# Loading two neighbouring chunks with one transfer of 64 KB rows in an RMS norm with ReLU

## The chip, the cores and the metric

The kernel runs on one core of a Trainium2 chip. The metric is the device time of one execution in microseconds (us). All runs quoted are with a granted clock of 1.00. The profiled span is the time from the first to the last instruction, some 1.3 us shorter than the device time.

## The reference

```python
def setup_inputs():
    batch, seq, dim = 16, 1024, 512
    x = randn(batch, seq, dim) as float32; gamma = ones(dim); eps = 1e-5

def reference(x, gamma, eps):
    rms = np.sqrt(np.mean(x ** 2, axis=-1, keepdims=True) + eps)
    return np.maximum(x / rms * gamma, 0)
```

There are 16384 rows of 512 numbers: 33.55 MB to read and as much to write.

## The kernel before

The 16384 rows are spread over 128 partitions, 128 rows of `x` on each, and worked off in eight chunks of K = 16 rows per partition (4.19 MB each). There is room for six chunks in the on-chip memory (`slots`), so chunks 6 and 7 go where 0 and 1 were, after those are stored. One queue, that of the issuing engine SP, takes all transfers in the order of this list:

```python
K = 16; G = 8; nslots = 6; room = nslots * K
order = [(L, 0, G), (L, G, G)] + [(L, i * K, K) for i in range(1, nslots)] + [
    (S, 0, K), (S, K, K), (L, room, K), (L, room + K, K),
    (S, 2 * K, 2 * K), (S, 4 * K, 2 * K), (S, room, K), (S, room + K, K)]
blocks = [(0, K), (K, K), (2 * K, 2 * K), (4 * K, 2 * K), (room, K), (room + K, K)]
```

`L` is a load, `S` a store; the numbers are the first row in each partition and the count. `blocks` says how a partition's rows lie in HBM: chunks 4 and 5 form one block, so a partition has 64 KB in one piece there (chunks 2 and 3 form another). Such a piece of one partition, as far as one transfer takes it, is called a row of 16, 32 or 64 KB below, not to be confused with the rows of `x`; it is one descriptor of the transfer and one packet of the profile, which counts 16 small packets more for each transfer's completion. The kernel before stores this block with one transfer of 64 KB rows, but loads it with two transfers of 32 KB rows.

Stores wait for VectorE. Two of them also wait for a count of VectorE's groups (`tick`, raised at the sixth of a group's eight rows). This wait is called the gate here:

```python
if kind == S:
    if order[m - 1][0] == L:
        nc.sync.wait_ge(tick, 6 if a == 0 else 11)
    nc.sync.wait_ge(done, (a + r) // G)
elif a >= room:
    take(nc.sync, sems[order.index((S, a - room, r))], 16)   # wait for the store, then load
transfer(m)
```

GpSimd waits for each load and announces its groups of G = 8 rows to ScalarE:

```python
if kind == L:
    take(nc.gpsimd, sems[m], 16)
    nc.gpsimd.sem_inc(ready, r // G)
```

ScalarE squares and sums each row of a group and takes the root (16 groups, numbered 0 to 15). VectorE takes the reciprocal, multiplies each row by it and by gamma, and clips a group at zero (groups 0 to 11); it does chunks 6 and 7 in two passes over the whole chunk, the second with a custom instruction.

## Time and profile before

| | kernel before |
|---|---|
| device time, median of 3 runs | 160.31 us (160.15 to 160.41) |
| profiled span | 158.9 us |
| VectorE busy | 129.4 us, 81% |
| ScalarE busy | 86.3 us, 54% |
| transfers, share of 16 DMA engines over the span | 98.3% |
| moved | 67.1 MB, 422 GB/s |

The two shares to set against each other are VectorE's and that of the transfers. The page's chain of waits names VectorE, because it follows instructions; whether it or the queue of transfers sets the end is what the prediction had to decide. In the profile's lines DVE is VectorE, ACT ScalarE, POOL GpSimd and SP the issuing engine; a q behind a name is that engine's sequencer, and L117 is line 117 of the kernel. ScalarE's waits of the kernel before (engine, line, what it waited for: us in total, times, longest):

```profile
ACT junk L130 <- POOLq L117: 17.4, 4, 10.4
```

POOLq L117 is GpSimd's announcement. The longest of the four waits, 10.4 us, is the one for chunk 6.

### The profile page before, as it was taken

How to read it: one execution, taken by the hardware profiler on the slowest of the kernel's cores; microseconds unless marked ns; L12 is line 12 of the kernel's file. 1: busy time of each engine (PE TensorE's matmuls, PEld its weight loads, DVE VectorE, ACT ScalarE, POOL GpSimd, SP SyncE). 2: the span in 40 equal slices, each digit the busy share in tenths (PEclk: the TensorE clock that was granted, in tenths of full speed). 3: DMA queues.
4: the chain of work that ended last, by engine and by line, in shares of the span. 5: the costliest groups of instructions: out<-in, count | busy, mean ns of one | idle time of the engine just before them, and what ended most of it. 6: DMA issues, size and time to landing. Idle time of an engine off the chain costs nothing.

```text
span 158.9 us, 902 instructions
## 1 busy us (share of the span) xinstructions
DVE 129.4 (81%) x128; ACT 86.3 (54%) x273; POOL 0.8 (0%) x6
## 2 busy tenths in 40 slices
DVE  0013999999999999999999999999999999996000
ACT  0388919889889989988930098898600000000000
POOL 1000000000000000000000000000000000000000
DMA  6999999999999999999999999996997998999996
GB/s 194 406 454 449 470 404 396 495 429 396 429 487 404 396 462 462 396 404 495 421 396 404 503 412 396 528 495 297 528 478 313 528 412 379 396 396 503 412 404 264
DMA packets 2168, 67.12 MB, mean 422 GB/s; under 512 B 244, under 2 KB 244, under 8 KB 248
## 3 DMA queue, kind: packets, MB, share of 16 engines
q1 hardware_dynamic: 2160, 67.11, 98.3%
q10 hardware_dynamic: 8, 0.01, 0.0%
HBM read 33.56 MB, written 33.55 MB: 422 GB/s over the span
## 4 chain that ended last, share of the span: by engine, by line
DVE 51%; issue 18%; DVEq 5%; ACT 3%; ACTq 0%; POOLq 0%
DVE slots L153 27%; DVE slots L170 11%; DVE slots L173 11%; DVEq L153 3%; ACT junk L130 3%; DVE rstd L148 1%; DVEq L143 1%; DVEq L148 0%; ACTq L130 0%; DVE rstd L168 0%; DVE slots L160 0%; ACT rms L135 0%; DVEq L162 0%; DVEq L172 0%; ACTq L135 0%
## 5 line engine op out<-in xcount | busy, mean ns | idle before, releaser
L130 ACT ACTIVATE junk<-slots 128x512 f32 x128 | 74.4, 581 | 21.9 <-POOLq L117 17.4
L153 DVE SCALAR_TENSOR_TENSOR slots<-slots,rstd,gamma_sb 128x512 f32 x96 | 64.7, 746 | 1.8 <-DVE rstd L148 1.8
L160 DVE TENSOR_SCALAR slots<-slots x12 | 27.5, 2294 | 0.4
L130 ACT ACTIVATION_READ_ACCUMULATOR junk<-slots x128 | 23.9, 186 | 0.0
L173 DVE CUSTOM_DVE_ANT_1 slots<-slots,gamma_sb 128x8192 f32<-128x8192 f32 x2 | 17.4, 8693 | 0.3
L170 DVE TENSOR_TENSOR slots<-slots,rstd 128x8192 f32<-128x8192 f32 x2 | 17.4, 8692 | 0.1
L148 DVE RECIPROCAL rstd<-rms x12 | 2.3, 195 | 5.4 <-ACT rms L135 5.4
L141 DVE LOAD_MASK_SELECT gamma_sb<-gseed x1 | 0.0, 14 | 8.0 <-DMA gseed<-in_gamma_dram 8.0
L135 ACT ACTIVATE rms<-ss,eps_sb x16 | 4.8, 301 | 1.8
L123 ACT ACT_TABLE_LOAD x1 | 1.3, 1283 | 4.0 <-issue 4.0
L141 DVE STREAM_SHUFFLE gamma_sb<-gseed 128x512 f32<-128x512 f32 x1 | 0.7, 717 | 0.0
L112 POOL MEMSET gseed<- 128x512 f32 x1 | 0.5, 525 | 1.9 <-POOLq L97 1.9
L168 DVE RECIPROCAL rstd<-rms 128x16 f32<-128x16 f32 x2 | 0.5, 246 | 0.0
L203 POOL MEMSET const-bfloat16-1.0<- 128x1 bf16 x1 | 0.1, 101 | 0.0
L203 POOL MEMSET const-uint8-127<- 128x1 uint8 x1 | 0.1, 101 | 0.0
L203 POOL MEMSET const-float32-0.0<- 128x1 f32 x1 | 0.1, 98 | 0.2 <-issue 0.2
L203 POOL MEMSET const-float32-1.0<- 128x1 f32 x1 | 0.1, 98 | 0.0
L113 POOL MEMSET eps_sb<- 128x1 f32 x1 | 0.1, 98 | 0.0
## 6 DMA issues: line engine op xcount, KB each, us to landing
slots<-in_x_dram SPq DMA_DIRECT2D x7, 4096.0 KB, 29.8
out_dram<-slots SPq DMA_DIRECT2D x4, 4096.0 KB, 17.4
slots<-in_x_dram SPq DMA_DIRECT2D x2, 2048.0 KB, 9.7
out_dram<-slots SPq DMA_DIRECT2D x2, 25.6
gseed<-in_gamma_dram ACTq DMA_DIRECT2D x1, 8.0 KB
```

The lines of the kernel that those rows point to most:

```text
L112: nc.gpsimd.memset(gseed, 0.0).then_inc(sem_z, 1)
L123: nc.scalar.preload_act_table(ACTF.Sqrt)
L130: a = nc.scalar.activation(out=junk[:, j, :], in_=slots[:, bass.ds(base + j * d, d)], func=ACTF.Square, accum_out=ss[:, bass.ds(col + j, 1)])
L135: nc.scalar.activation(out=rms[:, bass.ds(col, G)], in_=ss[:, bass.ds(col, G)], func=ACTF.Sqrt, bias=eps_sb, scale=inv_d).then_inc(sq, 1)
L141: nc.vector.stream_shuffle(gamma_sb, gseed, [0] * 32)
L143: with nc.vector.Fori(0, ndyn) as gi:
L148: nc.vector.reciprocal(out=rstd[:, bass.ds(col, G)], in_=rms[:, bass.ds(col, G)]).then_inc(sv, 1)
L153: r = nc.vector.scalar_tensor_tensor(out=row, in0=row, scalar=rstd[:, bass.ds(col + j, 1)], in1=gamma_sb, op0=ALU.mult, op1=ALU.mult)
L160: nc.vector.tensor_scalar_max(out=blk, in0=blk, scalar1=0.0).then_inc(done, 1)
L168: nc.vector.reciprocal(out=fac, in_=rms[:, i * K:(i + 1) * K]).then_inc(sv, 1)
L170: nc.vector.tensor_tensor(out=blk, in0=blk, in1=fac[:, :, None].to_broadcast([P, K, d]), op=ALU.mult).then_inc(sv, 1)
L173: nc.vector._custom_dve(dve_ops.TENSOR_MUL_SAT, out=blk, in0=blk, in1=gamma_sb[:, None, :].to_broadcast([P, K, d]), s0=float("inf"), s1=0. ...
```

## The change

The intent is to read chunks 4 and 5 as they lie in HBM, with half as many descriptors of twice the size and one transfer less.

```diff
-    order = [(L, 0, G), (L, G, G)] + [(L, i * K, K) for i in range(1, nslots)] + [
+    order = [(L, 0, G), (L, G, G)] + [(L, i * K, K) for i in range(1, 4)] + [(L, 4 * K, 2 * K)] + [
```

Nothing else changes. GpSimd now announces four groups at once, after the whole 8.39 MB have landed.

## The prediction

> **What bounds the kernel now.** I read the page's busy table and the forty slices first, then the queue of the engine that issues the transfers, then the packet counts of two stretches, and last the neighbourhood of chunk 4 on ScalarE and VectorE.
>
> The page of the kernel before (busy us and share of the 158.9 us span by engine; DMA busy in tenths per slice of 4 us; then queue: packets, MB, share of 16 engines):
>
> ```profile
> DVE 129.4 (81%) x128; ACT 86.3 (54%) x273; POOL 0.8 (0%) x6
> ...
> DVE  0013999999999999999999999999999999996000
> ACT  0388919889889989988930098898600000000000
> ...
> DMA  6999999999999999999999999996997998999996
> ...
> q1 hardware_dynamic: 2160, 67.11, 98.3%
> ```
>
> VectorE is full between its late start and its early end, and the chain of waits goes through it (51%). But the transfers are busy from the first slice to the last: 98.3% of all 16 engines over the whole span, on one queue. The kernel must move 33.55 MB in and 33.55 MB out, and does so with no hole. The chain of the page follows compute instructions and does not know that the transfers stand in a queue, so I trust the DMA row over it. Two checks follow.
>
> The issues, in order of time (start, length from first to last of a group), and the two last landings:
>
> ```profile
> 0.73 4.04 SPq L82 DMA_DIRECT2D slots<-in_x_dram  x7
> 58.55 0.82 SPq L82 DMA_DIRECT2D out_dram<-slots  x2
> 71.38 10.26 SPq L82 DMA_DIRECT2D slots<-in_x_dram  x2
> 98.45 47.41 SPq L82 DMA_DIRECT2D out_dram<-slots  x4
> ```
>
> All seven loads of the first six chunks are in the queue by 4.8 us, though the last of them lands only at 61.7 us (issued at 4.31 us, 57.4 us to landing). The last two stores are issued at 127.81 and 145.53 us with 21.4 and 13.4 us to landing, so they land at 149.2 and 158.9 us: 9.7 us apart. A 4 MB load in the middle of the first stretch takes the same time (25.17 MB land between the first packets at about 1.7 us and 61.7 us, so 9.7 to 10 us for each 4.19 MB). The last store therefore waited for the store ahead of it and not for VectorE, which had delivered its data at 145.5 us, 3.7 us before the store ahead had landed. The end is set by the transfer queue, with VectorE a few us behind it.
>
> **What the Trainium skill says.** All four are from its page "DMA: Bandwidth & Descriptors".
>
> Section "Where 436 GB/s comes from": 16 ports give 435.2 GB/s, which is 27.2 GB/s for each engine. The trace agrees, and has both descriptor sizes in it. The kernel before has rows of 32 KB in its loads and already has rows of 64 KB in the two stores of 8 MB. Packets of a stretch that holds 32 KB rows alone, bar a few at its edge (23 to 61 us), and of one that holds 64 KB rows alone (103 to 137 us):
>
> ```profile
> DMA packets 574, 16.74 MB, mean 441 GB/s; under 512 B 63, under 2 KB 63, under 8 KB 63
> ## 3 DMA queue, kind: packets, MB, share of 16 engines
> q1 hardware_dynamic: 574, 16.74, 102.2%
> ```
>
> ```profile
> DMA packets 240, 14.68 MB, mean 432 GB/s; under 512 B 16, under 2 KB 16, under 8 KB 16
> ## 3 DMA queue, kind: packets, MB, share of 16 engines
> q1 hardware_dynamic: 240, 14.68, 99.7%
> ```
>
> The small ones are completion writes. One row of 32 KB took 1.022 x 38 us x 16 / 511 = 1.216 us, or 26.9 GB/s; one of 64 KB took 0.997 x 34 us x 16 / 224 = 2.421 us, or 27.1 GB/s. (A packet counts where it starts, hence a share over 100%.) Doubling the row is worth 2 x 1.216 - 2.421 = 0.011 us, under half a per cent. That is the whole bandwidth effect that I can find.
>
> Section "Anatomy of one DMA" (written for the other descriptor path): a transfer has a fixed cost of about 2 us, most of it the receipt of the last write. It would be an estimate of the gain if that cost were paid between chunks 4 and 5. The trace says that it is not: 9.7 us for 4.19 MB is 432 GB/s, and no room for 2 us is left in it.
>
> Section "Queues, rings and completion order": each engine consumes the descriptors of a ring in order. This is why the next transfer starts while the receipt of the one before is still under way; the row of nines agrees.
>
> Section "Why a DMA increments its semaphore by 16 and not by 1": only the full count means that all has landed. So nothing of chunk 4 may be used before the last byte of chunk 5. No line of the profile of before can show that for a merged load, but it is the part of the change that costs.
>
> **The change part by part.** Removed: one of nine loads, its issue, its completion write on each of 16 engines, and one wait of GpSimd. Instruction order on the compute engines is the same in both kernels; only the issuing queue has one row fewer.
>
> (1) Rows. Chunks 4 and 5 were 256 rows of 32 KB, 16 for each engine; they become 128 rows of 64 KB, 8 for each. Per engine 8 x 0.011 = about 0.09 us less. With the 32 KB rows of the two last stores in place of the loads (0.989 x 18.5 x 16 / 241 = 1.215 us) it is 0.06 us. This lies on the path. Sum: -0.06 to -0.1 us.
>
> (2) The issue. The last issue of the first burst took 0.46 us on the queue's sequencer, 50 us before its data were due: 0 on the path.
>
> (3) The later landing of chunk 4. It landed at 52.0 us (the load before the last: about 3.8 us plus 48.2 us); now it lands with chunk 5 at 61.6 us. ScalarE needs it at 57.97 us:
>
> ```profile
> 57.97 0.60 ACT L130 ACTIVATE junk<-slots 128x512 f32 x1 [0.37 <-issue]
> 63.10 0.30 ACT L135 ACTIVATE rms<-ss,eps_sb  x1
> ```
>
> ```profile
> 70.07 0.20 DVE L148 RECIPROCAL rstd<-rms  x1
> ```
>
> ScalarE started chunk 6 at 91.20 us after a landing at 71.38 + 19.5 = 90.9 us, so it starts some 0.3 to 0.4 us after a landing. It would then begin group 8 at about 62.0 us in place of 57.97, a new wait of 4 us. One group takes 63.40 - 57.97 = 5.43 us, so its root is ready at 67.4 us. VectorE takes that root at 70.07 us (it goes one group of 8 rows each 7.98 us: 62.09, 70.07, 78.06). 2.6 us to spare, and ScalarE does a group in 5.8 us, so it gains 2.2 us on VectorE with each further one. After group 11 it would end near 84.9 us in place of 80.78 us, and then waits for chunk 6 until 91.2 us as before: the 4 us come out of its idle 10.4 us. Nothing of it reaches VectorE: 0 on the path.
>
> (4) The gates. The first store waits for VectorE's sixth group (58.55 us) and the third for its eleventh (98.45 us). Both follow VectorE's clock, which (3) leaves alone. Both stay ahead of the queue's running dry: 58.55 against 61.6 us, 98.45 against 100.5 us (load of chunk 7 issued near 81.3 us plus 19.3).
>
> Sum: 160.31 - 0.1 = 160.2 us.
>
> **The rivals.** (a) ScalarE's late start starves VectorE. The margin of (3) is 2.6 us. If the landing were 3 to 5 us later than I think, VectorE would lose 1 to 2 us there, the third store's gate (margin 2 us, of which the latency of an issue takes about 1) would open late, the queue would run dry, and the end would move by 1 to 2 us: 161 to 162 us. Against it: the load's end is a sum of bytes at a rate that the trace shows as constant.
>
> (b) Reading HBM in 64 KB rows is slower or faster than writing them. The trace has such rows only in stores; loads and stores of 32 KB took the same within 0.2%. If loads of 64 KB ran 3% slower, 19.3 us would become 19.9, the end 160.8 us, and the margin of (3) would shrink to 2 us, still enough.
>
> (c) The fixed cost of a transfer is really saved, 1 to 2 us: 158.5 to 159.3 us. The back-to-back landings speak against it.
>
> (d) The sixteen engines drift apart or closer by the longer rows, which moves the last landing by some tenths: 160.0 to 160.5 us. I cannot exclude it, and it is as large as the gain.
>
> **Range and chances.** Three runs of before lie in 0.26 us, more than the gain. (d) and this scatter give 159.9 to 160.6 us for 8 in 10. A change of 2% is 3.2 us; (a) and (c) would have to go beyond what I worked out. Same 0.98, faster 0.01, slower 0.01.
>
> **What would show it.** In the profile of the changed kernel: the q1 row with 2160 - 128 - 16 = 2016 packets at nearly the same share; ScalarE's first square of chunk 4 near 62.0 us with a wait on GpSimd's line of about 4 us, and its later wait for chunk 6 near 6 us in place of 10.4; VectorE's reciprocals still at 62.09, 70.07, 78.06 us; the last four issues where they were. A gap in the VectorE row near 67 to 70 us, a hole in the DMA row near 62 or 100 us, or two landings of chunk 6 and 7 moved by more than 0.3 us would show a step wrong, and a time below 159.5 or above 161 us the sum.

## The result

The changed kernel took 160.08 us in the median of 6 runs (160.02 to 160.37), the kernel before 160.28 us (160.15 to 160.50, 6 runs) beside it. The ratio is 0.999, with a 95% interval of 0.9978 to 1.0003. Ratios here are the mean time of one kernel's fast runs over that of the other's of the same rounds, so they are not quite the ratio of the medians. The prediction was 160.2 us, and "same" at 0.98.

The page of the changed kernel (rows as in the prediction):

```profile
DVE 129.4 (82%) x128; ACT 86.3 (54%) x273; POOL 0.8 (0%) x6
...
DVE  0013999999999999999999999999999999996000
ACT  0388919889889944998893098898600000000000
...
DMA  6999999999999699999999999996997969999996
...
q1 hardware_dynamic: 2016, 67.11, 98.4%
```

The packet count fell by 144, as foretold. VectorE's row is the same in every slice. ScalarE's row has a new dip of two slices (the 4s, about 55 to 63 us) and a shorter gap later (30 in place of 300). The 6 and 7 in the DMA row are no holes: a packet counts in the slice where it starts, and 64 KB packets are long.

The issues of the changed kernel in order of time:

```profile
0.73 3.53 SPq L82 DMA_DIRECT2D slots<-in_x_dram  x6
58.52 0.82 SPq L82 DMA_DIRECT2D out_dram<-slots  x2
71.21 10.40 SPq L82 DMA_DIRECT2D slots<-in_x_dram  x2
98.42 47.40 SPq L82 DMA_DIRECT2D out_dram<-slots  x4
```

One load is missing from the first group. Both gates open within 0.03 us of where they did. The last two stores are issued at 127.78 and 145.49 us, with 21.3 and 13.2 us to landing: they land at 149.1 and 158.7 us, still back to back.

The merged load was issued at 3.74 us, with 57.7 us to landing: 61.4 us. ScalarE and VectorE around it (start, duration, instruction; in brackets the idle time before it and what ended that):

```profile
61.84 0.60 ACT L130 ACTIVATE junk<-slots 128x512 f32 x1 [4.37 <-POOLq L117]
```

```profile
62.06 0.20 DVE L148 RECIPROCAL rstd<-rms  x1
...
70.04 0.19 DVE L148 RECIPROCAL rstd<-rms  x1
...
78.02 0.20 DVE L148 RECIPROCAL rstd<-rms  x1
```

ScalarE waits 4.37 us for chunk 4, which it did not before. VectorE's reciprocals stand where they stood. The wait is paid back within ScalarE's own idle time; its waits in the changed kernel:

```profile
ACT junk L130 <- POOLq L117: 17.3, 4, 6.4
```

The total is the same, and the longest wait, that for chunk 6, is 6.4 us in place of 10.4 us.

The rows themselves: packets of the changed kernel from 43 to 60 us, a stretch with the merged load alone:

```profile
DMA packets 112, 7.34 MB, mean 432 GB/s; under 512 B 0, under 2 KB 0, under 8 KB 0
## 3 DMA queue, kind: packets, MB, share of 16 engines
q1 hardware_dynamic: 112, 7.34, 99.7%
```

That is 0.997 x 17 us x 16 / 112 = 2.421 us for a 64 KB row read, the same figure as for the 64 KB rows written in the kernel before.

### The profile page after: what moved, and what is told of

It reads as the page before. It is cut to its first block, busy times and chain, and to the rows that moved or that the text cites. A ratio compares the mean times of both kernels' runs of the same rounds, so it can differ in the third digit from the quotient of the medians.

```text
span 158.8 us, 899 instructions
## 1 busy us (share of the span) xinstructions
DVE 129.4 (82%) x128; ACT 86.3 (54%) x273; POOL 0.8 (0%) x6
## 3 DMA queue, kind: packets, MB, share of 16 engines
q1 hardware_dynamic: 2016, 67.11, 98.4%
## 4 chain that ended last, share of the span: by engine, by line
DVE 51%; issue 19%; DVEq 5%; ACT 3%; ACTq 0%; POOLq 0%
DVE slots L153 27%; DVE slots L170 11%; DVE slots L173 11%; DVEq L153 3%; ACT junk L130 3%; DVE rstd L148 1%; DVEq L143 1%; DVEq L148 0%; ACTq L130 0%; DVE rstd L168 0%; DVE slots L160 0%; ACT rms L135 0%; DVEq L162 0%; DVEq L172 0%; ACTq L135 0%
## 6 DMA issues: line engine op xcount, KB each, us to landing
slots<-in_x_dram SPq DMA_DIRECT2D x1, 57.7
```

## The experiments

Theory: the end is the start of the queue plus the sum of all rows' times on each DMA engine, as long as the queue never runs dry. Merging shortens that sum by some hundredths of a microsecond, and the late landing of chunk 4 falls into slack. Rivals: a fixed cost of about 2 us for each transfer, as rival (c) of the prediction has it; VectorE's chain as what sets the end; a cost of the late landing that the longer rows hide.

VectorE's custom instruction could not be used in experiments. All of them have an ordinary one in its place, which is right here because gamma is not negative, and `base_split` and `base_merged` are their controls. All ten gave right results. They were made on three chips, each beside the kernel before (160.35, 160.32 and 160.28 us in the median), to which all ratios refer.

**base_split**, the kernel before with the substitute:

```diff
-        nc.vector._custom_dve(dve_ops.TENSOR_MUL_SAT, out=blk, in0=blk, in1=..., s0=float("inf"), s1=0.0)
+        nc.vector.scalar_tensor_tensor(out=blk, in0=blk, scalar=0.0, in1=..., op0=ALU.max, op1=ALU.mult)
```

> The kernel before, with the last VectorE pass of chunks 6 and 7 written as a scalar_tensor_tensor (max with 0, then times gamma; right because gamma is not negative here) in place of the custom instruction. It is the control for all other runs. Both theories: the pass takes 8.7 us as before and the time is that of the kernel before, 160.1 to 160.4 us. If the new pass were slower, the last stores would be issued late and this base could not be used.

Measured: 160.37 us (5 runs; the kernel before 160.35), ratio 0.9993 (0.998 to 1.0006). The substitute takes 8.69 us, as the custom instruction does. The control stands for the kernel before.

**base_merged**, the changed kernel with the substitute.

> The changed kernel with the same substitute. Queue theory (the sum of descriptor times on each of 16 engines sets the end): 0.06 to 0.1 us less than base_split, ratio 0.9994 to 0.9996, 112 data rows for each engine in place of 120. Rival (about 2 us of fixed cost saved with one transfer less): 158.3 to 159.3 us.

Measured: 160.31 us, ratio to the kernel before 0.9991 (0.9978 to 1.0004). The two controls differ by 0.0002, or 0.03 us, far inside the intervals. A fixed cost of 2 us is excluded; a gain of 0.06 us is too small to be seen in this way.

**late_only**, the late landing without the longer rows:

```diff
             take(nc.gpsimd, sems[m], 16)
-            nc.gpsimd.sem_inc(ready, r // G)
+            if a == 4 * K:
+                continue
+            nc.gpsimd.sem_inc(ready, 2 * per if a == 5 * K else r // G)
```

> Chunks 4 and 5 stay two loads of 32 KB rows, but GpSimd announces them together once both have landed: only the late landing of the change. Queue theory: the same time as base_split within 0.1 us, although ScalarE starts chunk 4 near 62 us and waits 4 us there. Rival (the late start costs, and the longer rows hide that): 0.5 to 2 us slower than base_merged.

Measured: 160.32 us, ratio 0.9991 (0.9979 to 1.0003). ScalarE started chunk 4 at 62.01 us after 4.45 us of waiting, and the time stayed. The late landing costs nothing by itself, so the longer rows hide no such cost.

**hold_tick7**, the announcement of chunks 4 and 5 held back further:

```diff
             take(nc.gpsimd, sems[m], 16)
+            if a == 4 * K:
+                nc.gpsimd.wait_ge(tick, 7)
             nc.gpsimd.sem_inc(ready, r // G)
```

> The changed kernel, but GpSimd announces chunks 4 and 5 only after VectorE's seventh group, near 66.5 us, so ScalarE has the root of group 8 near 72.3 us. If VectorE needs it at 70.07 us, as the prediction wrote (margin 2.6 us): VectorE loses 2.2 us, the third store is issued at 100.6 us, the queue runs dry for about 1.5 us and the time is near 161.5 us. If 70.07 us belongs to group 7 and group 8 is due at 78.06 us (margin 10.6 us): no change against base_merged, within 0.1 us.

Measured: 160.09 us, ratio 0.9979 (0.9966 to 0.9992). The interval lies just below 1 but overlaps that of base_merged, so I read no gain into it. ScalarE and VectorE in this run (source lines are shifted by two):

```profile
66.76 0.60 ACT L132 ACTIVATE junk<-slots 128x512 f32 x1 [9.27 <-POOLq L119]
```

```profile
70.03 0.19 DVE L150 RECIPROCAL rstd<-rms  x1
...
78.01 0.19 DVE L150 RECIPROCAL rstd<-rms  x1
```

ScalarE has the root of group 8 no earlier than 66.76 + 5.4 = 72.2 us, yet VectorE starts as ever at 70.03 us. What it takes there is therefore not group 8. The prediction's margin of 2.6 us is refuted.

**hold_tick8**, the same with `tick` 8.

> As hold_tick7, but chunks 4 and 5 are announced after VectorE's eighth group, near 74.5 us; ScalarE has the root of group 8 near 80.3 us. With the margin of 10.6 us (group 8 due at 78.06 us) this is the first hold that is too long: VectorE loses 2.2 us, its gate opens for the third store at 100.6 us in place of 98.4, the queue, which has emptied near 99.9 us, stands still until about 101.6 us, and the end moves by 1.5 to 2 us, to some 162 us. If VectorE's delay does not count, 160.2 us.

Measured: 161.66 us, ratio 1.0078 (1.0061 to 1.0095).

```profile
74.75 0.60 ACT L132 ACTIVATE junk<-slots 128x512 f32 x1 [17.29 <-POOLq L119]
```

```profile
80.33 0.20 DVE L150 RECIPROCAL rstd<-rms  x1 [2.22 <-ACT rms L137]
```

Now VectorE waits, 2.22 us, for the group that was due at 78 us. The third store is issued at 100.75 us, 2.5 us later than in base_merged (98.26 us), and the span grows by 1.4 us (160.4 against 159.0 us). The margin of the merged load is thus the one counted to 78.02 us: 78.02 - (61.84 + 5.43) = 10.7 us.

**merge_23**, the same change done to chunks 2 and 3 as well (a part of the line, against the changed kernel):

```diff
-[(L, i * K, K) for i in range(1, 4)] + [(L, 4 * K, 2 * K)]
+[(L, K, K), (L, 2 * K, 2 * K), (L, 4 * K, 2 * K)]
```

> The same change done to chunks 2 and 3 as well: one more pair in one load of 64 KB rows, which lands near 42.1 us. By descriptor time alone: another 0.06 to 0.1 us less than base_merged. By the waits: group 4 is due on VectorE at 46.1 us, ScalarE can start it near 42.5 and finish near 47.9, so VectorE loses 1.8 to 2 us for good; the third store's gate opens at 100.3 us, the queue stands still for 1 to 1.5 us (perhaps 0.3 us more near 61 us), and the time is 161.2 to 161.8 us.

Measured: 161.49 us, ratio 1.0067 (1.005 to 1.0084). The early part was as expected, with ScalarE at 42.56 us and VectorE late:

```profile
48.14 0.20 DVE L148 RECIPROCAL rstd<-rms  x1 [1.90 <-ACT rms L135]
```

The size was right, but not the places of the loss. The first store was issued at 60.57 us (58.36 in base_merged), and the queue ran dry there more than at the third store. Stretches of 1 us in this run (length, busy us and instructions of VectorE, ScalarE and GpSimd, clock, DMA share, GB/s):

```profile
60.00:61.00 1.00, 1.00 (x2) 1.00 (x3) 0.00 (x0) 1.00 0.01 0
...
79.00:80.00 1.00, 1.00 (x1) 1.00 (x5) 0.00 (x0) 1.00 1.95 524
...
100.00:101.00 1.00, 1.00 (x2) 1.00 (x5) 0.00 (x0) 1.00 0.68 295
```

In the changed kernel the stretch from 60 to 61 us has a share of 1.22. By the packet records an engine stood idle for 0.7 us on average at the first store, and for 0.2 us at the third, whose gate opened at 100.47 us. The 16 rows that started between 79 and 80 us took 1.95 us each, where the median row of 32 KB took 1.21 us; that is 0.7 us more, and why they were slow stays open. The three together exceed the 1.2 us by which the span grew, because the 16 engines also finished closer together (0.3 us apart, 1.0 us in base_merged). The same merge is free on chunks 4 and 5 and costs over 1 us on chunks 2 and 3. The loss begins with the time at which ScalarE needs the data; not all of it is explained.

**gate_12**, the third store issued one group later:

```diff
-                nc.sync.wait_ge(tick, 6 if a == 0 else 11)
+                nc.sync.wait_ge(tick, 6 if a == 0 else 12)
```

> The changed kernel, but the third store waits for VectorE's twelfth group in place of the eleventh (106.4 us in place of 98.4). Queue theory: a hole of about 7.5 us from 99.9 us on, and the end moves by as much, to 167 to 168 us, with VectorE's times unchanged. Rival (VectorE's chain sets the end, the queue has room): no more than 1 us slower.

Measured: 167.27 us, ratio 1.0439 (1.0421 to 1.0458). VectorE ended at 145.31 us, as before. The issue, and the queue around it in stretches of 1 us:

```profile
106.30 0.34 SPq L82 DMA_DIRECT2D out_dram<-slots  x1
```

```profile
98.00:99.00 1.00, 1.00 (x3) 1.00 (x5) 0.00 (x0) 1.00 1.22 524
99.00:100.00 1.00, 0.97 (x2) 1.00 (x4) 0.00 (x0) 1.00 0.01 0
...
106.00:107.00 1.00, 1.00 (x3) 1.00 (x4) 0.00 (x0) 1.00 0.00 0
107.00:108.00 1.00, 0.97 (x2) 0.89 (x5) 0.00 (x0) 1.00 2.46 1049
```

No packet starts for seven stretches, and the span grows by 7.0 us. With the same work on every compute engine, only the queue can have moved the end. The gate opened 8.0 us later than in base_merged and the span grew by 7.0, so about 1.0 us of lateness is free. hold_tick8, the other run with only the third store late, agrees: 2.5 - 1.4 us. (In merge_23 the difference is 2.2 - 1.2, but that run lost time in three places, so it is no clean measure.)

**fast_dve**, the opposite test, a faster VectorE (the edit in words):

```diff
-        nc.vector.tensor_tensor(blk * reciprocal), then the pass with gamma and max
+        16 x nc.vector.scalar_tensor_tensor(row * reciprocal * gamma), then nc.vector.tensor_scalar_max(blk)
```

> The changed kernel with chunks 6 and 7 done by VectorE row by row and a separate max, which by the durations of the first twelve groups takes about 15.9 us a chunk in place of 17.7, so VectorE ends 3 to 4 us earlier. Queue theory: the last store is issued 3 to 4 us earlier and lands at the same time; 160.2 us, within 0.1% of base_merged. Rival (VectorE's chain of waits, as the page has it, sets the end): 156.5 to 157.5 us.

Measured: 160.28 us, ratio 1.0 (0.9983 to 1.0017). VectorE ended at 140.92 us, 4.3 us earlier than in base_merged, and the last store was issued at 140.94 us:

```profile
140.94 0.33 SPq L82 DMA_DIRECT2D out_dram<-slots  x1
```

```profile
out_dram<-slots SPq DMA_DIRECT2D x1, 4096.0 KB, 17.9
```

It landed after 17.9 us, at 158.8 us, as in the kernels before (158.9 us) and after (158.7 us). VectorE's chain does not set the end.

**rows_16k**, all loads in pieces with 16 KB rows:

```diff
-    order = [(L, 0, G), (L, G, G)] + [(L, i * K, K) for i in range(1, nslots)] + [...
+    order = [(L, i * G, G) for i in range(nslots * per)] + [...      # and 6, 7 in halves, with one wait for each chunk
```

> The control base_split with all loads cut into pieces of 8 rows of x (16 KB rows in each partition, 2 MB a transfer): the opposite of the change, on all loads; 16 loads in place of 9. The packet records of the kernel before have 0.611 us for a 16 KB row and 1.213 us for one of 32 KB, so a pair costs 0.009 us more, 56 such pairs on each engine: queue theory 0.3 to 0.6 us slower than base_split. Rival (each transfer more costs its fixed 2 us): 14 us slower.

Measured: 160.69 us (the kernel before 160.28 beside it), ratio 1.0023 (1.0009 to 1.0037): 0.37 us for 56 rows more on each engine, or 6.6 ns for each split row (2.6 to 10.6 ns by the interval), and nothing like 14 us. This is against the kernel before; the control base_split stood at 0.9993 of it, on another chip.

**rows_16k_all**, loads and stores alike in such pieces.

> The control with all loads and all stores in pieces of 2 MB with 16 KB rows: 32 transfers in place of 15, 256 data rows on each engine in place of 120. Queue theory: by the packet durations 256 x 0.611 us against 155.2 us, 0.8 to 1.2 us slower than base_split. Rival (fixed cost for each transfer): 34 us slower. Rival (row length costs nothing): the same time.

Measured: 161.16 us, ratio 1.006 (1.0046 to 1.0074): 0.96 us for 136 rows more, or 7.1 ns each (5.4 to 8.7 ns by the interval). Packets from 24 to 56 us:

```profile
DMA packets 935, 13.75 MB, mean 430 GB/s; under 512 B 96, under 2 KB 96, under 8 KB 96
## 3 DMA queue, kind: packets, MB, share of 16 engines
q1 hardware_dynamic: 935, 13.75, 100.8%
```

A 16 KB row took 1.008 x 32 us x 16 / 839 = 0.615 us, or 26.6 GB/s against 27.1 for one of 64 KB. The cost of shorter pieces is real. Whether it belongs to the row or to the transfer these two times can't tell: both runs add eight rows on each engine with every further transfer (56 with 7, 136 with 17), so 0.05 to 0.06 us for a transfer fits them as well. The packet records speak for the row. In the trace of the kernel before the median row of 16, 32 and 64 KB took 0.611, 1.213 and 2.418 us, so a split costs 2 x 0.611 - 1.213 = 0.009 or 2 x 1.213 - 2.418 = 0.008 us, and a completion write took 0.009 us. By the rows alone that makes 0.5 and 1.2 us, near the upper ends of the two intervals (0.59 and 1.19 us), and leaves nothing for the transfers.

## Why the prediction was right

**The bound.** It held that the queue sets the end with VectorE a few us behind. gate_12 shows it from one side (a hole of seven us, VectorE untouched, 7.0 us more), fast_dve from the other (VectorE 4.3 us earlier, no gain).

**Step (1), the rows.** Right in kind, and at the upper edge in size. The term was -0.06 to -0.1 us from eight pairs at up to 0.011 us. The two runs with split rows lost 0.05 to 0.06 us for each transfer that came with its eight rows, and the change takes away one such transfer, so it is worth 0.05 to 0.06 us whichever of the two the cost belongs to. The figure of 0.011 us is a difference of means, in which a few slow rows count; the medians of the packet records give 0.008 us. (The prediction's 27.2 GB/s for each engine is an estimate, the 435.2 GB/s of the page that it cites divided by 16.) That the changed kernel itself was measured 0.2 us lower in the median is not evidence for more: its interval includes no change, and the controls with the same edit differ by 0.03 us.

**Step (2), the issue.** Nothing on the path, as told: the first group of issues is 0.5 us shorter, and the first gate is where it was.

**Step (3), the later landing.** The conclusion held, and late_only shows it alone. The times came out as worked: landing at 61.4 us against 61.6, start at 61.84 against 62.0, the later wait 6.4 us against "near 6". But one reading in it was wrong: "VectorE takes that root at 70.07 us", with "2.6 us to spare". The reciprocal at 70.07 us is that of group 7. Counted in steps of 7.98 us from the first at 14.21 us it is the eighth, and the eighth has number 7; group 8, the first of chunk 4, was due at 78.06 us. The margin is 10.7 us. hold_tick7 spent 4.9 us of it and lost nothing; hold_tick8 spent 12.9 and lost 2.2 us on VectorE. The error was on the safe side. Rival (a) was therefore much weaker than written: a landing 3 to 5 us later would not have moved the end.

**Step (4), the gates.** The spare of 2 us, of which the latency of an issue takes about 1, was right for the third store: gate_12 and hold_tick8 leave 1.0 to 1.1 us free. For the first store the prediction set the issue at 58.55 us against a landing at 61.6 us, which would be 3 us. The queue runs dry when the last rows end, not when they have landed: by the packet records of the kernel before, the engines ended these loads between 60.6 and 61.1 us. In merge_23, 2.2 us of lateness there did stop the queue.

**The rivals.** (b), a different rate of reading 64 KB rows, is settled by the 2.421 us that both directions took. (c), a fixed cost of a transfer, is settled by rows_16k_all, where 17 transfers more cost 0.96 us together, rows included. The queue does not wait for a landing: in the changed kernel sixteen rows of 32 KB, those of the store behind the merged load, started between 60 and 61 us, and the load landed at 61.4 us. (d), a scatter between the engines of some tenths, was not tested on its own, but the packet records show its size. The last completion writes of the 16 engines lie 0.82 us apart in the kernel before and 0.68 us in the changed one, but 0.88 and 0.96 us in their two controls, and the first of them comes between 157.5 and 157.6 us in all four. So the scatter is as large as forecast, and no effect of the longer rows on it is seen. The repeated runs of one kernel spread by up to 0.5 us, and what causes that stays open.

No run beat both kernels by more than this spread. Of the span of the changed kernel, 98.4% is busy transfer time, at 26.9 to 27.1 GB/s an engine for rows of 32 and 64 KB.

## What to carry to other kernels

Before merging transfers, look whether the queue ever runs empty between them. If it does not, the fixed cost is already hidden, and only a small difference is left, here 0.05 to 0.06 us for a transfer with its eight rows on each engine. Then count for the merged data when the first consumer needs them, group by group and from zero: the same merge was free for chunks 4 and 5, with 10.7 us to spare, and cost over 1 us for chunks 2 and 3.

## What the Trainium skill lacked or had wrong

- "DMA: Bandwidth & Descriptors", section "Anatomy of one DMA", gives about 2 us plus bytes over a rate for a transfer. It is a fit for one transfer and on the other descriptor path; the page does not say what a further transfer costs in a queue that is never empty. Here 17 more of them, with 136 more rows on each engine, cost 0.96 us together, 0.06 us each, rows included.
- The same page, section "Specifications", calls 512 B and more enough for full rate and gives no figures for long rows of equal total size. Here 16, 32 and 64 KB rows took 0.615, 1.216 and 2.421 us, or 26.6, 26.9 and 27.1 GB/s for an engine. Loads and stores took the same at 32 and 64 KB; 16 KB was read off loads alone.
- The same section gives about 0.6 us to the first byte for transfers issued from the SP engine, and does not say from where it counts. In gate_12 the store was issued at 106.30 us into an empty queue, and its first packets started between 107.1 and 107.3 us, so 0.8 to 1.0 us after the start of the issue and 0.5 to 0.7 us after its end (it took 0.34 us). The second agrees with the page. A store has to be issued 0.8 to 1.0 us before the queue runs dry.
